# Layer norm behind a matmul: how the last row tile gets its shift

## The chip, the core and the metric

The kernel runs on one core of a Trainium2 chip. The metric is device time in microseconds of one launch. Three runs of the kernel before gave a median of 249.34 us (249.0 to 249.43).

## What is computed

A 2048x2048 matmul in fp32 inputs, and a layer norm over each row of the result:

```python
x = np.matmul(a, b)                              # 2048 x 2048 x 2048, fp32
mean = np.mean(x, axis=-1, keepdims=True)
var = np.var(x, axis=-1, keepdims=True)
normalized = (x - mean) / np.sqrt(var + eps)
return (gamma * normalized + beta).astype(np.float32)
```

## The kernel before

The 2048 output rows are sixteen row tiles of 128 rows. A row tile has four column blocks (q = 0 to 3) of 512 columns, and each is summed over sixteen k-tiles in one PSUM bank, with f16 copies of `a` (transposed) and `b` as operands. Everything is written in the order in which it is to run; there is no scheduler that moves work. Each engine takes its instructions in program order.

The first seven row tiles are worked on together while `b` arrives (blocks 1 and 0, then 2 and 3). From row tile 7 on, a row tile is finished before the next begins: `quarter` runs the sixteen products of a block, `evacuate` copies the bank to SBUF on ScalarE and takes the block's statistics on VectorE. `close` joins the statistics and puts the normalization into a backlog, which VectorE works off while TensorE goes on with the next tile.

The last row tile (15) has no next tile to hide behind, so it is treated apart. Its blocks 0 to 2 are multiplied by gamma as soon as they are there (`scaled`, L356), so that after the last product only `x*gamma*rstd + (beta - mean*rstd*gamma)` is left for them. Its block 3 isn't copied out of PSUM. After its last product, `finish_row` runs:

- `bn_stats` of block 3 from PSUM (L363), then in `stats` the aggregation into `mv` (mean, variance; L103), the addition of eps (`ve`, L105) and the square root on ScalarE (`sq`, L107).
- Eight products of zeros on TensorE (`filler`, L364 and L232).
- Block 3 centred and multiplied by gamma (L366), the reciprocal (`rstd`, L128), `nm = -mean*rstd` (L371).
- `nm`, a column of 128 values, is turned into a row by a product with a unit matrix (L374), copied by ScalarE into row 0 of `lead`, whose row 1 is ones (L375). Two products of two rows each (L379) then give `w[q] = nm*gamma + beta` for q = 1 and 2, in PSUM. Their moving operands, gamma above beta, are loaded into `rows_gb` earlier (L350).
- Block 3 is scaled and stored (L118, L124); for q = 0 VectorE itself computes `shift = gamma*nm + beta` (L384); then blocks 0, 1 and 2 get `x*rstd + w[q]` (L389) and are stored one by one by SP (L124).

All of these fp32 products appear in the trace as two matmul records each.

Of the kernel before, what the change touches and what calls it, by code (L numbers as in the profile page):

```python
# [9 lines left out]
FP32 = mybir.dt.float32  # L10
FP16 = mybir.dt.float16
AluOp = mybir.AluOpType
ActFn = mybir.ActivationFunctionType
# [3 lines left out]
def kernel(  # L17
# [9 lines left out]
    nc = tc.nc  # L27
    P = 128
# [5 lines left out]
    NB = 512  # L34
    n_nb = N // NB
    NH = N // 2
# [13 lines left out]
    konst = ctx.enter_context(tc.tile_pool(name="konst", bufs=1))  # L50
    bpool = ctx.enter_context(tc.tile_pool(name="bpool", bufs=1))
    stg = ctx.enter_context(tc.tile_pool(name="stg", bufs=6))
# [3 lines left out]
    stat = ctx.enter_context(tc.tile_pool(name="stat", bufs=8))  # L56
    psum = ctx.enter_context(tc.tile_pool(name="psum", bufs=8, space=bass.MemoryType.PSUM))
# [5 lines left out]
    eps_t = konst.tile([P, 1], FP32)  # L63
    gate = konst.tile([P, 1], FP32)
    gamma_b = konst.tile([P, N], FP32)
    beta_b = konst.tile([P, N], FP32)
# [3 lines left out]
    xs = [None] * n_mt  # L70
# [3 lines left out]
    def bank(name):  # L74
        return psum.tile([P, NB], FP32, tag="ps", name=name)
# [25 lines left out]
    def stats(i):  # L101
        mv = stat.tile([P, 2], FP32, tag="mv", name=f"mv{i}")
        nc.vector.bn_aggr(mv, bnst[i])  # L103
        ve = stat.tile([P, 1], FP32, tag="ve", name=f"ve{i}")
        nc.vector.tensor_tensor(ve, mv[:, 1:2], eps_t, AluOp.add)  # L105
        sq = stat.tile([P, 1], FP32, tag="sq", name=f"sq{i}")
        nc.scalar.activation(sq, ve, ActFn.Sqrt)  # L107
        return mv, sq

    def centre(i, q, mv):  # L110
# [5 lines left out]
    def scale(i, q, rstd):  # L116
        qs = ds(q * NB, NB)
        nc.vector.scalar_tensor_tensor(  # L118
            xs[i][:, qs], xs[i][:, qs], rstd, beta_b[:, qs],
            AluOp.mult, AluOp.add)  # L120

    def store(i, q0, nq):
        s = ds(q0 * NB, nq * NB)
        nc.sync.dma_start(out[ts(i, P), s], xs[i][:, s])  # L124

    def inv(i, sq):
        rstd = stat.tile([P, 1], FP32, tag="rstd", name=f"rstd{i}")
        nc.vector.reciprocal(rstd, sq)  # L128
        return rstd
# [100 lines left out]
    def filler(n, to=None):  # L230
        for _ in range(n):
            nc.tensor.matmul(warm if to is None else to, zeros[:, 0:P], zeros, start=True, stop=True)  # L232
# [22 lines left out]
    for what in arrivals:  # L255
# [9 lines left out]
        i = what[1]  # L265
# [73 lines left out]
        nc.gpsimd.dma_start(a16[i], a[ts(i, P), :])  # L339


    rows_gb = [stg.tile([2, 2, NB], FP32, tag="st", name=f"gb{h}") for h in (0, 1)]
    ident32 = stg.tile([P, P], FP32, tag="st", name="ident32")
    nc.vector.tensor_copy(ident32, ident)
    shift = stg.tile([P, NB], FP32, tag="st", name="shift")
    lead = konst.tile([2, P], FP32)
    nc.vector.memset(lead, 1.0)
    for h in (0, 1):
        for m, vec in enumerate((gamma, beta)):
            nc.sync.dma_start(  # L350
                rows_gb[h][m:m + 1, :, :],
                vec[ds(h * NH, NH)].rearrange("(o t n) -> o t n", o=1, t=2))

    def scaled(i, q):
        qs = ds(q * NB, NB)
# [2 lines left out]
    def finish_row(i):  # L358


        q3 = ds(3 * NB, NB)
        last_acc = acc[i, 3]
        nc.vector.bn_stats(bnst[i][:, 3, :], last_acc)  # L363
        filler(8, bank("warm2"))  # L364
        mv, sq = stats(i)
        nc.vector.scalar_tensor_tensor(  # L366
            xs[i][:, q3], last_acc, mv[:, 0:1], gamma_b[:, q3],
            AluOp.subtract, AluOp.mult)
        rstd = inv(i, sq)
        nm = stat.tile([P, 1], FP32, tag="nm", name="nm")  # L370
        nc.vector.scalar_tensor_tensor(  # L371
            nm, mv[:, 0:1], -1.0, rstd, AluOp.mult, AluOp.mult)
        nm_ps = psum.tile([1, P], FP32, tag="ps", name="nm_ps")
        nc.tensor.matmul(nm_ps, nm, ident32, start=True, stop=True)  # L374
        nc.scalar.copy(lead[0:1, :], nm_ps)  # L375
        w = {}
        for q in (1, 2):
            w[q] = bank(f"w{q}")
            nc.tensor.matmul(  # L379
                w[q], lead, rows_gb[q // 2][:, q % 2, :], start=True, stop=True)  # L380
        scale(i, 3, rstd)
        store(i, 3, 1)
        q0 = ds(0, NB)
        nc.vector.scalar_tensor_tensor(  # L384
            shift, gamma_b[:, q0], nm, beta_b[:, q0], AluOp.mult, AluOp.add)
        w[0] = shift
        for q in range(3):
            qs = ds(q * NB, NB)
            nc.vector.scalar_tensor_tensor(  # L389
                xs[i][:, qs], xs[i][:, qs], rstd, w[q], AluOp.mult, AluOp.add)  # L390
            store(i, q, 1)
# [5 lines left out]
    def close(i):  # L397
        mv, sq = stats(i)
        queue_norm(i, mv, sq)
        drain(1)  # L400
# [15 lines left out]
    for i in range(n_first, n_mt):  # L416
        last = i == n_mt - 1
        turn_ahead(i + 4)
        for q in range(2 if i < R else 0, n_nb):
            quarter(i, q)  # L420
            if last and q == n_nb - 1:
                break
            evacuate(i, q)
            if q < n_nb - 1:
                drain(1)
            if last:
                scaled(i, q)
        if last:
            drain(len(backlog))
            finish_row(i)  # L430
        else:
            close(i)
# [35 lines left out]
```

## Time and profile before

| | |
|---|---|
| median of three runs | 249.34 us (249.0 to 249.43) |
| the profiled execution | 249.5 us |
| its span, first to last instruction | 247.7 us |
| mean granted TensorE clock in it | 0.989 |
| TensorE busy with matmuls | 240.7 us (97%) |
| VectorE busy | 173.0 us (70%) |
| ScalarE busy | 56.9 us (23%) |

A profile is of one execution. Durations in it are microseconds from the span's start unless marked ns. "PE" is TensorE's matmuls, "PEld" its weight loads, DVE is VectorE, ACT is ScalarE, POOL is GpSimd, SP is the engine that issues the DMAs ("SPq" its queue). A group reads: line, engine, operation, output<-inputs, partitions x elements, type, count, then busy time and the mean ns of one, then the idle time of the engine ahead of it and what ended it. Matmuls are pipelined, so their records overlap, and a busy PE is not PE at its peak.

### The profile page before, as it was taken

Reading aid. Unit: us, or ns where it says so; the run is one execution under the profiler, and the core shown is the slowest. Engines: PE = TensorE matmul, PEld = TensorE weight load, DVE = VectorE, ACT = ScalarE, POOL = GpSimd, SP = SyncE. Lnnn points to the kernel's source line nnn. Section 1 sums busy time; section 2 is a strip of 40 time slices with the busy share of each in tenths; the row PEclk is TensorE's granted clock in tenths of the full one; section 3 lists DMA queues with packets and bytes.
Section 4 is the critical chain, followed back from the end, with each engine's and each line's share of the span. In section 5 each row is a group of like instructions: output and inputs, shape, how many; then the busy total and the mean of one; then the engine's idle time right before and its main releaser. Section 6 shows DMA issues by size and latency. Waiting matters only on the chain.

```text
span 247.7 us, 3055 instructions
## 1 busy us (share of the span) xinstructions
PE 240.7 (97%) x1175; PEld 110.5 (45%) x1175; DVE 173.0 (70%) x307; ACT 56.9 (23%) x101; POOL 5.6 (2%) x15
## 2 busy tenths in 40 slices
PE   8999999999999999999999999999999999999983
PEld 3445555444444444444444444444444444444430
DVE  1454555965799999999999492856658292947873
ACT  2276446400013312221112121212111121112100
POOL 0000000000030000000000000000000000000000
PEclk9999999999999999999999999999999999999995
DMA  5999999999999239999999979180903122120404
GB/s 147 331 390 385 379 363 389 387 386 385 390 350 210 99 128 221 201 281 252 120 285 324 252 186 266 68 219 3 253 1 125 47 85 85 67 102 3 171 0 169
DMA packets 37846, 52.64 MB, mean 213 GB/s; under 512 B 20292, under 2 KB 20292, under 8 KB 37576
## 3 DMA queue, kind: packets, MB, share of 16 engines
q1 hardware_dynamic: 36536, 47.73, 58.1%
q0 software_dynamic: 1296, 4.72, 12.0%
q8 instruction: 9, 0.15, 0.2%
q14 instruction: 5, 0.04, 0.1%
HBM read 35.67 MB, written 16.78 MB: 212 GB/s over the span
## 4 chain that ended last, share of the span: by engine, by line
PE 92%; DMA 3%; SPq 2%; DVE 1%; issue 0%; ACT 0%
PE acc L86 88%; DMA st<-in_a_dram 3%; PE tps L239 2%; PE w L379 1%; SPq L187 1%; SPq L201 1%; DVE x L389 0%; DVE bnst L363 0%; DVE x L366 0%; DVE a16s L189 0%; PE nm_ps L374 0%; DVE mv L103 0%; ACT lead L375 0%; DVE nm L371 0%; DVE ve L105 0%
## 5 line engine op out<-in xcount | busy, mean ns | idle before, releaser
L86 PE MATMUL acc<-b,at 128*128 128x512 f16 x1024 | 224.1, 379 | 0.0
L86 PEld LDWEIGHTS <-at 128*128 128x128 f16 x1024 | 99.5, 98 | 117.8 <-ACT at L241 1.1
L97 DVE BATCH_NORM_STATS2 bnst<-x 128x6 f32<-128x512 f32 x56 | 38.4, 687 | 36.7 <-ACT x L96 36.7
L96 ACT COPY x<-acc 128x512 f32<-128x512 f32 x56 | 32.7, 585 | 129.5 <-PE acc L86 129.4
L118 DVE SCALAR_TENSOR_TENSOR x<-x,rstd,beta_b 128x512 f32<-128x512 f32 x61 | 43.1, 748 | 0.5
L112 DVE SCALAR_TENSOR_TENSOR x<-x,mv,gamma_b 128x512 f32<-128x512 f32 x60 | 42.1, 744 | 0.0
L208 DVE CAST b<-stb 128x1024 f16<-128x1024 f32 x30 | 20.8, 692 | 14.9 <-DMA stb<-in_b_dram 14.5
L241 ACT COPY at<-tps 128x512 f16<-128x512 f16 (+1 forms) x19 | 15.0, 787 | 21.2 <-PE tps L239 21.2
L232 PE MATMUL warm<-zeros 128*128 128x512 f16 x33 | 11.0, 466 | 1.2 <-DVE zeros L153 1.2
L197 DVE CAST a16s<-sta 128x1024 f16<-128x1024 f32 x9 | 6.2, 694 | 6.1 <-DMA sta<-in_a_dram 6.1
L107 ACT ACTIVATE sq<-ve 128x1 f32<-128x1 f32 x16 | 3.2, 203 | 31.3 <-DVE ve L105 31.3
L239 PEld LDWEIGHTS <-a16s 128*128 128x128 f16 x112 | 7.6, 99 | 6.2 <-DVE a16s L189 2.9
L239 PE MATMUL tps<-ident,a16s 128*128 128x128 f16 x112 | 9.6, 222 | 0.6 <-DVE a16s L189 0.5
L189 DVE CAST a16s<-st 128x512 f16<-128x512 f32 x10 | 4.3, 425 | 6.3 <-DMA st<-in_a_dram 6.3
L339 POOL DMA_DIRECT2D a<-in_a_dram x9 | 4.9, 547 | 70.0 <-DMA at<-a 69.7
L232 PEld LDWEIGHTS <-zeros 128*128 128x128 f16 x33 | 3.5, 114 | 5.3 <-issue 2.4
L327 DVE BATCH_NORM_STATS2 bnst<-x 128x6 f32<-128x512 f32 x7 | 4.9, 695 | 0.2
L325 DVE TENSOR_TENSOR x<-acc,x 128x512 f32<-128x512 f32 x7 | 4.8, 681 | 0.0
L103 DVE BATCH_NORM_AGGREGATE mv<-bnst 128x2 f32<-128x24 f32 x16 | 4.2, 264 | 0.5
L297 ACT COPY x<-acc 128x512 f32<-128x512 f32 x7 | 3.5, 632 | 0.0
L202 DVE CAST b<-st 128x512 f16<-128x512 f32 x4 | 1.7, 428 | 2.3 <-DMA st<-in_b_dram 2.3
L105 DVE TENSOR_TENSOR ve<-mv,eps_t 128x1 f32<-128x1 f32 x16 | 2.6, 160 | 0.5
(26 smaller groups left out, 17.4 us busy)
## 6 DMA issues: line engine op xcount, KB each, us to landing
stb<-in_b_dram SPq DMA_DIRECT2D x30, 512.0 KB, 7.4
out_dram<-x SPq DMA_DIRECT2D x30, 512.0 KB, 3.0
sta<-in_a_dram SPq DMA_DIRECT2D x9, 512.0 KB, 7.5
a<-in_a_dram POOLq DMA_DIRECT2D x9, 512.0 KB, 8.0
st<-in_a_dram SPq DMA_DIRECT2D x10, 256.0 KB, 7.0
st<-in_b_dram SPq DMA_DIRECT2D x4, 256.0 KB, 5.8
gamma_b<-in_gamma_dram SPq DMA_DIRECT2D x1, 1024.0 KB, 9.4
beta_b<-in_beta_dram SPq DMA_DIRECT2D x1, 1024.0 KB, 11.3
```

Source lines behind the costliest of these rows:

```text
L86: nc.tensor.matmul(acc[i, q], at(i)[:, kt, :], b16[:, kt, ds(q * NB, NB)], start=first, stop=last,)
L96: nc.scalar.copy(xs[i][:, qs], acc[i, q])
L97: nc.vector.bn_stats(bnst[i][:, q, :], xs[i][:, qs])
L112: nc.vector.scalar_tensor_tensor(xs[i][:, qs], xs[i][:, qs], mv[:, 0:1], gamma_b[:, qs], AluOp.subtract, AluOp.mult)
L118: nc.vector.scalar_tensor_tensor(xs[i][:, qs], xs[i][:, qs], rstd, beta_b[:, qs], AluOp.mult, AluOp.add)
L197: nc.vector.tensor_copy(held["a"][:, ds(i % KC, 2), :], st)
L208: nc.vector.tensor_copy(b16[:, k:k + 2, ds(q * NB, NB)], st)
L232: nc.tensor.matmul(warm if to is None else to, zeros[:, 0:P], zeros, start=True, stop=True)
L239: nc.tensor.transpose(t_ps[:, m, j, :], a16_of[i, c][:, ts(j, P)], ident)
L241: nc.scalar.copy(pair[i0 // 2][:, ds(i0 % 2, n), ds(c * KC, KC), :], t_ps)
L327: nc.vector.bn_stats(bnst[p][:, 0, :], xs[p][:, 0:NB])
L339: nc.gpsimd.dma_start(a16[i], a[ts(i, P), :])
```

## The change

In `stats`, which all row tiles use, eps is no longer added by VectorE but given to the square root as its bias. In `finish_row` the fillers go. Ahead of the statistics' joining, TensorE gets two products of one row each that put beta into the banks of `w[1]` and `w[2]` and leave them open for accumulation. `nm` is laid on the diagonal of a 128x128 tile by ScalarE (a scaled copy of the unit matrix), and the product of that diagonal with gamma (128 rows deep) is added to the banks. The product that turned `nm` into a row, the copy into `lead` and the four loads of `rows_gb` are gone. The centring of block 3 is done in two halves, one ahead of the reciprocal and one behind `nm`. The last three blocks are finished in the order 1, 2, 0.

```diff
     def stats(i):
         mv = stat.tile([P, 2], FP32, tag="mv", name=f"mv{i}")
         nc.vector.bn_aggr(mv, bnst[i])
-        ve = stat.tile([P, 1], FP32, tag="ve", name=f"ve{i}")
-        nc.vector.tensor_tensor(ve, mv[:, 1:2], eps_t, AluOp.add)
         sq = stat.tile([P, 1], FP32, tag="sq", name=f"sq{i}")
-        nc.scalar.activation(sq, ve, ActFn.Sqrt)
+        nc.scalar.activation(sq, mv[:, 1:2], ActFn.Sqrt, bias=eps_t)
         return mv, sq
...
-    rows_gb = [stg.tile([2, 2, NB], FP32, tag="st", name=f"gb{h}") for h in (0, 1)]
     ident32 = stg.tile([P, P], FP32, tag="st", name="ident32")
     nc.vector.tensor_copy(ident32, ident)
     shift = stg.tile([P, NB], FP32, tag="st", name="shift")
-    lead = konst.tile([2, P], FP32)
-    nc.vector.memset(lead, 1.0)
-    for h in (0, 1):
-        for m, vec in enumerate((gamma, beta)):
-            nc.sync.dma_start(
-                rows_gb[h][m:m + 1, :, :],
-                vec[ds(h * NH, NH)].rearrange("(o t n) -> o t n", o=1, t=2))
+    diag = stg.tile([P, P], FP32, tag="st", name="diag")
+    ones = konst.tile([1, P], FP32)
+    nc.vector.memset(ones, 1.0)
...
         last_acc = acc[i, 3]
         nc.vector.bn_stats(bnst[i][:, 3, :], last_acc)
-        filler(8, bank("warm2"))
+        w = {0: shift}
+        for q in (1, 2):
+            w[q] = bank(f"w{q}")
+            nc.tensor.matmul(
+                w[q], ones, beta_b[0:1, ds(q * NB, NB)], start=True, stop=False)
         mv, sq = stats(i)
-        nc.vector.scalar_tensor_tensor(
-            xs[i][:, q3], last_acc, mv[:, 0:1], gamma_b[:, q3],
-            AluOp.subtract, AluOp.mult)
+
+        def centre_part(c0, c):
+            qs = ds(3 * NB + c0, c)
+            nc.vector.scalar_tensor_tensor(
+                xs[i][:, qs], last_acc[:, ds(c0, c)], mv[:, 0:1], gamma_b[:, qs],
+                AluOp.subtract, AluOp.mult)
+
+        centre_part(0, NB // 2)
         rstd = inv(i, sq)
         nm = stat.tile([P, 1], FP32, tag="nm", name="nm")
         nc.vector.scalar_tensor_tensor(
             nm, mv[:, 0:1], -1.0, rstd, AluOp.mult, AluOp.mult)
-        nm_ps = psum.tile([1, P], FP32, tag="ps", name="nm_ps")
-        nc.tensor.matmul(nm_ps, nm, ident32, start=True, stop=True)
-        nc.scalar.copy(lead[0:1, :], nm_ps)
-        w = {}
+        nc.scalar.mul(diag, ident32, nm)
         for q in (1, 2):
-            w[q] = bank(f"w{q}")
             nc.tensor.matmul(
-                w[q], lead, rows_gb[q // 2][:, q % 2, :], start=True, stop=True)
+                w[q], diag, gamma_b[:, ds(q * NB, NB)], start=False, stop=True)
+        centre_part(NB // 2, NB // 2)
         scale(i, 3, rstd)
         store(i, 3, 1)
-        q0 = ds(0, NB)
         nc.vector.scalar_tensor_tensor(
-            shift, gamma_b[:, q0], nm, beta_b[:, q0], AluOp.mult, AluOp.add)
-        w[0] = shift
-        for q in range(3):
+            shift, gamma_b[:, 0:NB], nm, beta_b[:, 0:NB], AluOp.mult, AluOp.add)
+        for q in (1, 2, 0):
             qs = ds(q * NB, NB)
```

## The prediction

> **What bounds the kernel now.** I read the page first. Its busy line and the row of the big product say that TensorE sets the time almost to the end; the clock row says that something happens to TensorE only in the last slice.
>
> ```profile
> span 247.7 us, 3055 instructions
> ...
> PE 240.7 (97%) x1175; PEld 110.5 (45%) x1175; DVE 173.0 (70%) x307; ACT 56.9 (23%) x101; POOL 5.6 (2%) x15
> ...
> PEclk9999999999999999999999999999999999999995
> ...
> L86 PE MATMUL acc<-b,at 128*128 128x512 f16 x1024 | 224.1, 379 | 0.0
> ```
>
> The chain that ended last shows one unbroken piece of L86 from 40.99 to 237.84. So what the change does in the other fifteen rows (one 0.16 us add less in each `stats`, L105) and at the start (four small loads fewer) lies beside TensorE's work and is worth nothing. Everything is decided after the last product, at 237.85. There the chain, asked for its last 10 us, goes on like this (start, duration, what):
>
> ```profile
> 240.14 0.39 PE nm_ps L374 x2
> 240.53 0.02 issue
> 240.55 0.26 ACT lead L375
> 240.81 0.04 issue
> 240.86 2.59 PE w L379 x4
> 243.45 0.03 issue
> 243.47 0.75 DVE x L389
> ```
>
> It ends through the two products `w` on TensorE: the last L389 waits for `w[2]`. The timeline of the same stretch gives VectorE's steps (start, duration):
>
> ```profile
> 237.87 0.70 DVE L363 BATCH_NORM_STATS2 bnst<-acc 128x6 f32<-128x512 f32 x1 [1.41 <-PE acc L86]
> ...
> 238.60 0.27 DVE L103 BATCH_NORM_AGGREGATE mv<-bnst 128x2 f32<-128x24 f32 x1
> 238.90 0.16 DVE L105 TENSOR_TENSOR ve<-mv,eps_t 128x1 f32<-128x1 f32 x1
> 238.98 0.74 DVE L366 SCALAR_TENSOR_TENSOR x<-acc,mv,gamma_b 128x512 f32<-128x512 f32 x1
> 239.16 0.20 ACT L107 ACTIVATE sq<-ve 128x1 f32<-128x1 f32 x1 [4.15 <-DVE ve L105]
> 239.64 0.15 DVE L128 RECIPROCAL rstd<-sq 128x1 f32<-128x1 f32 x1
> 239.83 0.16 DVE L371 SCALAR_TENSOR_TENSOR nm<-mv,rstd 128x1 f32<-128x1 f32 x1
> 239.91 0.74 DVE L118 SCALAR_TENSOR_TENSOR x<-x,rstd,beta_b 128x512 f32<-128x512 f32 x1
> ...
> 240.57 0.74 DVE L384 SCALAR_TENSOR_TENSOR shift<-gamma_b,nm,beta_b 128x512 f32<-128x512 f32 x1
> ```
>
> To be read here: an instruction that needs nothing of the one before it starts earlier than that one ends (239.91 to 240.57 is 0.66 for a row of 0.74); one that needs its result starts 0.03 to 0.04 after its end. So a 512-wide pass costs 0.66, or 0.78 ahead of a dependant; a one-column step costs 0.08, or 0.19. The square root was done at 239.36, but the reciprocal waited until 239.64 behind L366.
>
> VectorE could have begun the last L389 at 242.69 (the second began at 242.02) and began it at 243.47. Two rows tell why: a timeline answer for TensorE alone around 241.2, and the table by stretches (TensorE busy is the first figure after the length, the granted clock stands after POOL).
>
> ```profile
> 240.86 1.12 PE L379 MATMUL w<-gb,lead 2*128 2x512 f32 x2 [0.34 <-ACT lead L375]
> ```
>
> ```profile
> 238.70:242.11 3.41, 2.49 (x9) 0.97 (x8) 3.31 (x9) 0.46 (x2) 0.00 (x0) 1.00 0.18 67
> 239.56:242.11 2.55, 1.63 (x6) 0.78 (x6) 2.48 (x7) 0.25 (x1) 0.00 (x0) 1.00 0.24 90
> 242.11:243.45 1.34, 1.32 (x2) 0.00 (x0) 0.66 (x1) 0.00 (x0) 0.00 (x0) 0.50 0.44 162
> ```
>
> At full clock one `w` is ready 1.12 after its start (0.69 for the first pass, 0.43 for the second); the second `w` would follow 0.86 later, at 242.84. The clock fell to half at 242.11 and made that 243.45. At full clock the last step would have ended at 243.63 instead of 244.22: 0.59 of the profiled end is the clock.
>
> **The sum.** From the end of the last VectorE step (244.22) to the end of the span (247.70) there are 3.48 for the last store, and the profiled execution took 249.50, so 1.80 lie outside the span. This execution is 0.16 above the median of 249.34. A time below is therefore the end of the last L389 plus 5.28.
>
> Statistics and root. The add L105 goes; the root reads `mv` itself. It started 0.10 after the add's end, so now 0.10 after 238.87: 238.97 to 239.17. A bias read from a tile in place of a constant has no row; I take nothing, and 0.12 is free anyway, since the reciprocal comes later. Centring half 1 starts at 238.90. Its cost: 512 columns hold VectorE 0.66 and a one-column step 0.08, which on a straight line gives 0.37 for 256; with 0.02 for caution 0.39. The reciprocal starts at 239.29 instead of 239.64, `nm` at 239.48 and ends at 239.64. That is 0.35 earlier.
>
> Diagonal. Removed from the path: the product L374 and the copy L375, that is from the end of `nm` (239.99) to the start of `w` (240.86), 0.87. In their place ScalarE writes 128x128. Its bounds are 0.20 (128x1, L107) and 0.59 (128x512, L96); a straight line gives 0.30 and I take that. Start 0.10 after `nm`: 239.74 to 240.04, TensorE at 240.09. This is 0.77 earlier than before; at the upper bound 0.48.
>
> The products with gamma. Four passes of 512 fp32 columns as before, but 128 rows deep instead of 2. L374 streams a 128-row fp32 operand twice 128 columns wide in 0.39, of which an isolated f16 product of that width takes 0.22, so depth shows no surcharge. Its weights, 128x128 fp32, have no row: L379's 2x128 took 0.18, the f16 128x128 0.10. I take 0.18; were it 0.36, both `w` come 0.18 later (later loads hide behind 0.43 passes) and the end is about 0.2 later, 249.0. The Trainium skill ("TensorE: Matmul & The Clock Gate", LDWEIGHTS) has a load depend on columns and not on rows, which would make that surcharge nothing. So `w[1]` is ready at 241.21 and `w[2]` at 242.07.
>
> The beta products. Two fp32 products of one row stand ahead, four passes of 0.43 from 237.85: done at 239.56, or 239.73 with the drain. The eight fillers that they replace ended at 239.56. Nothing on the path waits for them; cover is 0.36 to 240.09. At half clock they would end near 241.4 and push both `w` by 1.3.
>
> VectorE to the end. Half 2 of the centring starts behind `nm` at 239.56, and its full length is 0.74 less 0.27, so 0.47: 240.03. `scale` L118 needs it, 240.07; it ends 0.16 later than before, and so the first store, which has three others behind it. The shift starts at 240.73, and since the next step no longer needs it, that one may start at 241.39. Column block 1: 241.39 (`w[1]` has been ready 0.18). Block 2: 242.06 by VectorE, 242.11 by `w[2]`. Block 0: 242.78, ending at 243.53. The stores follow 0.67 apart; SP needs 0.33 for one, and before, the two at 242.13 and 242.79 were as close, so I charge nothing, up to 0.1. Against 244.22 that is 0.69: **248.81**, 0.53 (0.2%) below the median. About 0.6 of it is the clock avoided and only 0.1 the shorter path: VectorE itself has no gap left.
>
> **The rivals.**
>
> *The clock falls during the products (slower).* Before, eight f16 products kept TensorE streaming until 239.56, and 2.55 later the clock was cut although the rows have it busy for 1.63 of that. If narrow fp32 work counts little as load, the changed kernel's load ends at 237.85 and the same 2.55 gives a cut at 240.41, inside the products. Checked on before: 0.56 of streaming left at 242.11 (242.84 less a drain of 0.17: an f16 record lasts 0.38, the next follows after 0.21) doubled predicts 243.40, measured 243.45. With a cut at 240.41, `w[1]` comes at 241.84 and `w[2]` at 243.56; block 2 starts at 243.60, block 0 at 244.27, end 245.02: 250.3, slower by 0.9. It decides from a cut before about 241.2: then `w[2]` is at 242.77 and the end where it was. For it: one-row products replace full ones. Against: if fp32 work counts as busy, only 0.5 of idle time is left between 237.85 and 242.07, where 0.92 was.
> The Trainium skill (same page, The HAM clock gate) says that the clock is decided in free-running windows of about 3.4 us, and is cut after an idle one. The trace agrees on the grid: the first fillers start 0.43 apart until about 6.6 and 0.22 after it, and 242.11 less 6.6 is 69 such windows; it disagrees on "idle", with 2.49 busy of the last 3.41. By that grid the decisions here fall at 238.70 and 242.11, the second just behind my products: 248.8. As the page has the grid at another place in every execution, it would also allow 250.3.
>
> *Nothing measurable.* Where before's clock falls late, before ends at 243.63 and gains only 0.10. Likewise a cut at 241.2 in the changed kernel. Time 249.0 to 249.5. For it: the three runs span 0.43, which is less than the clock's 0.59. Against: the median stands 0.4 above such an unhindered run (249.50 less 0.59 is 248.91).
>
> *ScalarE loads a table for the scaled copy.* L107 shows one load of 1.28, none between its sixteen roots and the copies around them. If the scaling brought one, `w[2]` would be ready at 243.35 and the end 244.8, 250.1. A small chance.
>
> *The change doesn't shorten the root's wait* because the reciprocal still stands behind a half of the centring: included, 0.05 at most.
>
> **How the numbers follow.** A measurement of this kernel can tell about 0.2%, 0.5 us, from no change. Forecast (clock holds): 0.62, of which 0.47 beyond that bound and 0.15 within, as 0.53 hardly passes it. Cut during the products: 0.22, of which 0.20 slower and 0.02 within. Nothing measurable: 0.12 (0.03, 0.08, 0.01). Table load: 0.04, slower. Sums: 0.50, 0.25, 0.25. Range: from 248.4, which is the forecast less the 0.43 by which the three runs differ, up to 250.0, which takes in the dearer weights, the late cut and about half of the early ones; some 0.15 to 0.2 lies outside.
>
> **What would show it.** Right: no L105; the reciprocal near 239.3 if the last product ends at 237.85; `w` with gamma starting 0.45 after `nm` ends; three passes of block 1, 2, 0 at 0.67 spacing with no wait on TensorE; the granted clock 1.00 until past 242.0; last step ending 243.5. Wrong: a wait of block 2 on `w`, with the clock row at 0.50 earlier; TensorE still on beta after 240; a table load at the scaled copy; a diagonal that takes 0.5.

## The result and the profile after

The changed kernel takes 250.78 us (median of 20 runs, 248.94 to 251.91); the kernel before, measured beside it, 249.09 (248.34 to 250.06). The ratio is 1.006 with a 95% interval of 1.0046 to 1.0075: slower by 0.6%, where 0.2% faster was forecast. The median hides two groups. Twelve of the twenty have a mean granted TensorE clock of 0.990 or less (below, such a run is called cut) and take 250.5 to 251.9; the other eight have 0.995 to 0.998 and take 248.9 to 249.7. So two questions are to be answered: why the first group exists, and why the second is not at 248.8.

The profiled execution took 250.9 and belongs to the first group. Its page begins:

```profile
span 248.9 us, 3024 instructions
...
PEclk9999999999999999999999999999999999999987
```

The chain behind the last big product (start, duration, what):

```profile
237.75 0.71 DVE bnst L356
...
239.37 0.17 DVE nm L373
239.54 0.02 issue
239.56 0.41 ACT diag L375
239.97 0.04 issue
240.02 3.57 PE w L377 x4
243.59 0.02 issue
243.61 0.75 DVE x L386
244.36 0.66 DVEq L460
```

Up to the start of the products with gamma it goes as forecast: 237.75 to 240.02 is 2.27 (forecast 237.87 to 240.09, 2.22). Then the four passes take 3.57 instead of the 1.98 of full clock. The timeline shows what VectorE makes of it (the last column is its wait):

```profile
241.91 0.75 DVE L386 SCALAR_TENSOR_TENSOR x<-x,rstd,w 128x512 f32<-128x512 f32 x1 [0.53 <-PE w L377]
243.61 0.75 DVE L386 SCALAR_TENSOR_TENSOR x<-x,rstd,w 128x512 f32<-128x512 f32 x1 [0.96 <-PE w L377]
```

Against the sum of the prediction, the 2.09 too few in this execution (250.90 less 248.81) lie here:

| part | forecast | measured | difference |
|---|---|---|---|
| last big product ends at | 237.83 | 237.71 | -0.12 |
| from there to the end of the last VectorE step | 5.70 | 7.31 | +1.61 |
| from there to the end of the span | 3.48 | 3.91 | +0.43 |
| outside the span | 1.80 | 1.96 | +0.16 |

The last two rows are in the second group of runs as well. Of the changed kernel run again, the profiled execution kept its clock (249.54). Its timeline is the forecast one: products with gamma in 1.98, no waits worth naming, and the last step ending 5.74 behind the last big product (forecast 5.70). Behind that step it still takes 3.93 to the end of the span and 2.00 outside it:

```profile
239.72 0.40 ACT L375 ACTIVATE diag<-ident,nm 128x128 f32<-128x128 f32 x1 [0.43 <-DVE nm L373]
...
240.18 1.98 PE L377 MATMUL w<-gamma_b,diag 128*128 128x512 f32 x4 [0.40 <-ACT diag L375]
...
242.87 0.75 DVE L386 SCALAR_TENSOR_TENSOR x<-x,rstd,shift 128x512 f32<-128x512 f32 x1
```

### The profile page after: what moved, and what is told of

It reads as the page before. It is cut to its first block, busy times and chain, and to the rows that moved or that the text cites. A ratio compares the mean times of both kernels' runs of the same rounds, so it can differ in the third digit from the quotient of the medians.

```text
span 248.9 us, 3024 instructions
## 1 busy us (share of the span) xinstructions
PE 240.9 (97%) x1169; PEld 110.5 (44%) x1169; DVE 170.4 (68%) x292; ACT 58.9 (24%) x101; POOL 5.6 (2%) x15
## 4 chain that ended last, share of the span: by engine, by line
PE 92%; DMA 3%; SPq 2%; DVE 1%; issue 0%; DVEq 0%; ACT 0%
PE acc L86 88%; DMA st<-in_a_dram 3%; PE tps L237 2%; PE w L377 1%; SPq L185 1%; SPq L199 1%; DVE x L386 0%; DVE bnst L356 0%; DVEq L460 0%; DVE x L366 0%; DVE a16s L187 0%; ACT diag L375 0%; DVE mv L103 0%; DVE nm L373 0%; DVE rstd L126 0%
## 5 line engine op out<-in xcount | busy, mean ns | idle before, releaser
L105 ACT ACTIVATE sq<-mv,eps_t 128x1 f32<-128x1 f32 x16 | 4.7, 295 | 22.5 <-DVE mv L103 22.5
L230 PE MATMUL warm<-zeros 128*128 128x512 f16 x25 | 8.5, 463 | 1.2 <-DVE zeros L151 1.2
L230 PEld LDWEIGHTS <-zeros 128*128 128x128 f16 x25 | 2.6, 114 | 4.5 <-issue 2.4
L377 PE MATMUL w<-gamma_b,diag 128*128 128x512 f32 x4 | 3.6, 1045 | 0.4 <-ACT diag L375 0.4
```

Of the source, the lines that this page charges most:

```text
L377: nc.tensor.matmul(w[q], diag, gamma_b[:, ds(q * NB, NB)], start=False, stop=True)
```

## Experiments on the clock

**The changed kernel once more**, without an edit.

> The changed kernel once more, for its spread beside the others. Theory N (one-row fp32 products do not count as load, so the clock is cut at the first 3.41 us window that holds too little of the wide work before 237.8): some runs near 249.4, where the cut falls behind the products, and more of them at 250.5 to 251.9, where it falls inside; median 250 to 251. Rival F (any fp32 product counts little): the same. Rival S (the loss is the order of the stores at the end, not the clock): all runs within 0.5 of one another.

Measured: 249.56 (248.86 to 250.74), ratio 1.0021 (1.0003 to 1.0038). The runs are 1.88 apart, so rival S falls. Three of twelve were cut, against twelve of twenty in the first set. A third time (below) it was five of six, 250.59. So the loss of a set of runs depends on how many of them are cut; in all, 20 of 38 were. Two of the three here, at 249.65 and 249.81, stand close to the uncut ones; the prediction has a cut behind about 241.2 come too late to cost anything.

**Only the depth of the beta products** (e1_deep_beta): as many passes, the same values in the banks.

```diff
-                w[q], ones, beta_b[0:1, ds(q * NB, NB)], start=True, stop=False)
+                w[q], ident32, beta_b[:, ds(q * NB, NB)], start=True, stop=False)
```

> Only the depth of the beta products is changed: the 128-row unit matrix times the broadcast beta in place of one row of ones times one row of beta; same passes, same results. Theory N: now all the work counts, no window ahead of the products' end is poor, so no run above 250, median 248.8 to 249.4, granted clock 1.00 until past 242. Rival F (fp32 as such counts little): as the changed kernel, 250.8 median, clock cut inside the products. Rival S (stores): as the changed kernel.

Measured: 249.63 (249.12 to 250.46), ratio 1.0027 (1.001 to 1.0043), all twelve clocks 0.994 or more. The forecast of the clock held, that of the time (248.8 to 249.4) did not: there is a loss that isn't the clock.

**The kernel before with narrow fillers** (e2_before_narrow):

```diff
-        filler(8, bank("warm2"))
+        warm2 = bank("warm2")
+        for q in (1, 2):
+            nc.tensor.matmul(
+                warm2, lead[0:1, :], beta_b[0:1, ds(q * NB, NB)], start=True, stop=True)
```

> The kernel before with its eight f16 fillers replaced by two one-row fp32 products of the same length (four passes), results unused. Theory N: the clock is cut up to 1.7 us earlier, inside the two products of w; median 0.5 to 1.5 above the kernel before, single runs up to 252. Rival F: the same as theory N. Rival S: unchanged, 249.1.

Measured: 249.85 (248.41 to 250.55), ratio 1.0026 (1.0006 to 1.0047), nine of twelve clocks at 0.990 or less, where the kernel before beside it had 3 of 35. That is 0.65 above the kernel before by the ratio and 0.86 by the medians, inside the 0.5 to 1.5 of theory N; no run came near 252.

The tables by stretches of these kernels settle what counts. Each stretch is the 3.41 us ahead of a place where the clock could change. The first figure after the length is TensorE's busy time; the third from the end is the clock granted in the stretch itself, so what was decided at its end stands in the line below. First the changed kernel (cut at 240.28):

```profile
236.87:240.28 3.41, 3.01 (x9) 1.12 (x8) 2.39 (x7) 0.70 (x2) 0.00 (x0) 1.00 0.00 0
240.28:243.70 3.42, 3.29 (x4) 0.71 (x3) 1.93 (x4) 0.00 (x0) 0.00 (x0) 0.50 0.26 98
243.70:247.11 3.41, 0.00 (x0) 0.00 (x0) 1.32 (x2) 0.00 (x0) 0.00 (x0) 1.00 0.59 210
```

Then e1_deep_beta, whose clock was kept behind the first of these two stretches:

```profile
237.89:241.30 3.41, 2.82 (x8) 1.04 (x7) 3.12 (x8) 0.70 (x2) 0.00 (x0) 1.00 0.00 0
241.30:244.72 3.42, 0.99 (x3) 0.16 (x1) 2.43 (x4) 0.00 (x0) 0.00 (x0) 1.00 0.64 235
```

And e2_before_narrow:

```profile
240.31:243.72 3.41, 3.17 (x4) 1.16 (x4) 2.19 (x4) 0.19 (x1) 0.00 (x0) 0.50 0.41 154
243.72:247.13 3.41, 0.61 (x1) 0.00 (x0) 0.75 (x1) 0.00 (x0) 0.00 (x0) 0.50 0.41 154
```

TensorE is busy for 3.01 of 3.41 with one-row products among it, and the clock is cut; it is busy for 2.82 with 128-row products, and the clock is kept. At half clock, 3.29 of 128-row products bring it back to 1.00 (243.70); 3.17 of two-row products do not (243.72). So narrow fp32 products keep TensorE busy but count for little or nothing as load, while fp32 as such counts: rival F of the expectations falls.

The profiled execution of e3_order (next) makes it sharper. TensorE is busy for 3.01 there too, from 238.42 to 241.83, and the clock is kept; 1.62 of it is 128-row products, next to 1.10 in the cut stretch of the changed kernel. That the values count instead (a row of ones against a unit matrix) doesn't fit: in the changed kernel the clock rose at 4.76, when TensorE had run nothing but products of zeros.

Six kernels with the 128-row beta products and the three f16 versions below had no clock under 0.992 in 99 runs.

**The order 1, 0, 2** (e3_order):

```diff
-        for q in (1, 2, 0):
+        for q in (1, 0, 2):
```

> The changed kernel with the last blocks in the order 1, 0, 2 instead of 1, 2, 0: block 0, whose shift needs no product, is done while w[2] is still being computed. Theory N: where the clock is cut inside the products, the end comes 0.67 earlier (the pass of block 0 fits into the wait of 0.96); where it isn't, nothing changes; median 250.2 to 250.5. Rival S: the stores stand further apart, the gain is in all runs alike, 0.3 or more.

Measured: 250.06 (249.68 to 251.56), ratio 1.0053 (1.0036 to 1.007). Its profiled execution wasn't cut; the last step ended 5.64 behind the last big product, 0.10 less than in the other order. Four of twelve runs were cut, and what they gain can't be told from these numbers. Rival S's gain in all runs is not there. Instead 0.33 more lies outside the span (median 2.41 against 2.08), for which see the next section. As a test of the order it is inconclusive.

## Experiments on the loss that is not the clock

Here four times of the last store are compared, read from the trace: its issue, its landing (the last of its semaphore events), the end of the span and the run's end. "Outside" is the median over the runs of time less span; "fetch" is the start of the last 8 KB code fetch (a DMA packet that brings instructions), counted from the end of the span. "SP" is the number of SP's records, that is the length of its program.

| kernel | issue to landing | landing to end | outside | SP | fetch |
|---|---|---|---|---|---|
| before | 2.45 | 1.00 | 1.76 | 207 | +1.00 |
| changed | 2.64 | 1.25 | 2.08 | 202 | +1.86 |
| e1_deep_beta | 2.67 | 1.25 | 2.09 | 202 | +1.87 |
| e2_before_narrow | 2.45 | 1.02 | 1.80 | 207 | +1.03 |
| e3_order | 2.76 | 1.25 | 2.41 | 201 | +2.21 |
| e4_loads_back | 2.65 | 1.01 | 1.79 | 208 | +0.54 |
| e7_before_more_loads | 2.44 | 1.73 | 1.78 | 213 | -0.30 |
| e12_loads_by_act | 2.66 | 1.00 | 2.10 | 202 | +1.88 |
| e14_eight_loads | 2.66 | 1.73 | 1.78 | 211 | -0.22 |

Three things are longer in the changed kernel. *Issue to landing* is 0.2 to 0.3 longer wherever the last two stores are 0.66 apart (in e2_before_narrow the last one is issued 1.70 behind the one ahead of it, in before 1.45). *Landing to end:* behind the last store SP waits for its DMA semaphores one by one in a fixed order, each wait 0.06 behind the one before. In before the last store lands on the sixth of eight, in the changed kernel on the second. The line of SP's last drains shows the end of that round; first before, then the changed kernel:

```profile
L463 SPq DRAIN  x3: 7/7/7, 246.9 to 247.2; - x3
```

```profile
L460 SPq DRAIN  x3: 7/7/7, 248.1 to 248.4; - x3
```

The landings were at 246.70 and 247.69, so it is 0.2 in the one and 0.4 in the other. *Outside* is taken up below.

**The four loads put back** (e4_loads_back, on e1_deep_beta; the tile of ones, which nothing reads any more, is gone in this and the later versions with 128-row beta products):

```diff
+    rows_gb = [stg.tile([2, 2, NB], FP32, tag="st", name=f"gb{h}") for h in (0, 1)]
...
+    for h in (0, 1):
+        for m, vec in enumerate((gamma, beta)):
+            nc.sync.dma_start(
+                rows_gb[h][m:m + 1, :, :],
+                vec[ds(h * NH, NH)].rearrange("(o t n) -> o t n", o=1, t=2))
```

> e1_deep_beta with the four small loads of gamma and beta put back; nothing reads what they bring. Theory W (at the end SP waits for its DMA semaphores one by one in a fixed order, 0.06 us each; four loads fewer let the last store land on a semaphore that stands four places earlier in that order): the time from the last store's landing to the end of the span falls from 1.25 to 1.00, so the median falls by 0.25 against e1_deep_beta. Rival (the longer tail is the crowding of the last stores): 1.25 stays, no change.

Measured: 249.30, ratio 0.9996 (0.998 to 1.0012), against 1.0027 for e1_deep_beta. 1.01 behind the landing, as theory W says; and the time outside fell to 1.79, which it did not foretell. By these two times, loads that nothing reads are worth 0.54 here.

**The additions put back** (e5_adds_back, on e1_deep_beta), and **both** (e6_both_back):

```diff
+        if i == n_mt - 1:
             nc.scalar.activation(sq, mv[:, 1:2], ActFn.Sqrt, bias=eps_t)
+        else:
+            ve = stat.tile([P, 1], FP32, tag="ve", name=f"ve{i}")
+            nc.vector.tensor_tensor(ve, mv[:, 1:2], eps_t, AluOp.add)
+            nc.scalar.activation(sq, ve, ActFn.Sqrt)
```

> e1_deep_beta with the addition of eps put back on VectorE in the first fifteen row tiles; the last one keeps the bias. Theory C (the time outside the span is longer because VectorE's shorter program ends just ahead of a boundary at which 8 KB of code are fetched, so the fetch that the kernel before made at 232 us now comes after the last instruction): a fetch near 232 in the trace again, the time outside the span falls from 2.07 to about 1.76, the median by 0.3 against e1_deep_beta. Rival (the time outside belongs to the last stores or to SP): 2.07 stays. The path behind the last product is the same in both.

> e4_loads_back and e5_adds_back together: the path of the changed kernel with 128-row beta products, the loads and the additions of before. Theories W and C: 0.55 below e1_deep_beta, 248.6 to 249.1, level with or 0.1 to 0.4 below the kernel before. Rivals: as e1_deep_beta, about 249.6.

Measured: e5_adds_back 249.50, ratio 1.0009 (0.9991 to 1.0026); a code fetch at 231.8 is there again, and the time outside is 2.05. Theory C has fallen: VectorE's fetch and the time outside have nothing to do with one another. e6_both_back 249.30, ratio 0.9996 (0.998 to 1.0013), the same as e4_loads_back. The additions are worth nothing, as forecast.

**The kernel before with eight loads instead of four** (e7_before_more_loads; the second four go to tiles of their own, unread):

```diff
     for h in (0, 1):
         for m, vec in enumerate((gamma, beta)):
...
+            nc.sync.dma_start(
+                idle_gb[h][m:m + 1, :, :],
+                vec[ds(h * NH, NH)].rearrange("(o t n) -> o t n", o=1, t=2))
```

> The kernel before with the four small loads doubled to eight, the second four unread. Theory W: the last store lands four semaphores on, so the time from its landing to the end of the span is 1.25 instead of 1.00 and the median 0.25 above the kernel before. Rival (crowded stores): 1.00, no change.

Measured: 250.10, ratio 1.0038 (1.002 to 1.0055). The store lands on the second semaphore, as foretold, but 1.73 instead of 1.25 lie behind it. Most of the 0.48 is one step of SP among its last waits, 0.40 long instead of 0.06 (246.79 to 247.19), and a code fetch now starts inside the span, at 247.83. The pause ends 0.64 ahead of the fetch's packet, and from the packet on SP is as quick as in before (0.45 from its last drain to its last wait, 0.44 there). So the pause comes with the fetch, but the packet itself is not what SP stands still for; what it is stays open.

**The changed kernel and the four loads, nothing else** (e10_after_third without an edit, e11_after_loads with the edit of e4_loads_back on the changed kernel):

> The changed kernel a third time, beside the next one. Time outside the span 2.07; from the last store's landing to the end of the span 1.25; some runs with a granted clock of 0.990 or less (cut inside the products), the rest near 249.5.

> The changed kernel, one-row beta products kept, with the four small loads put back, unread. Theory W plus theory D (the time outside the span is SP's: its shorter program reaches the boundary of an 8 KB code fetch later behind the kernel's end): 1.00 instead of 1.25 behind the landing, 1.78 instead of 2.07 outside, so 0.55 below the changed kernel at the same clock; the share of cut clocks unchanged. Rival (VectorE's program sets the time outside): 2.07 stays and only 0.25 is gained.

Measured side by side: 250.59, ratio 1.0063 (1.0042 to 1.0084), and 248.95, ratio 1.001 (0.9995 to 1.0025). In e11_after_loads 1.01 lie behind the landing (246.09 to 247.10) and 1.86 outside. Five of six and five of eleven runs were cut, so the medians differ by more than the loads are worth; the uncut runs of e11_after_loads take 248.4 to 249.0.

**Turn or length** (on e1_deep_beta: the four loads issued by ScalarE, and eight loads on SP):

```diff
-            nc.sync.dma_start(
+            nc.scalar.dma_start(
```

```diff
+            for _ in (0, 1):
                 nc.sync.dma_start(
```

> e4_loads_back, but the four unread loads are issued by ScalarE's queue, so SP's program is as short as in the changed kernel. Theory D (the time outside the span follows the length of SP's program): 2.07 outside again. Rival (it follows the semaphore on which the last store lands, or the loads themselves): 1.78 outside. The time from the last landing to the end of the span tells by itself whether loads of another queue move the semaphores: 1.00 if so, 1.25 if not.

> e1_deep_beta with eight unread loads on SP instead of four: a whole turn of the eight semaphores, so the last store lands where it does with none, but SP's program is longer. Theory W: 1.25 behind the landing again, and as in e7_before_more_loads perhaps 0.5 more where the code fetch falls inside the span. Theory D: 1.78 outside, not 2.07. Rival for both (a load count as such gives the gain): 1.00 and 1.78.

Measured: e12_loads_by_act 249.01, ratio 0.9995 (0.9975 to 1.0014), 1.00 behind the landing and 2.10 outside. Loads of another queue turn the semaphores just as well, but the time outside stays with SP's short program. e14_eight_loads 249.82, ratio 1.0027 (1.0007 to 1.0048): a whole turn, the store on the second semaphore again, 1.73 behind the landing and 1.78 outside. The fetch is inside the span again, and again one step of SP is long (0.38, between two of its drains) and ends 0.64 ahead of the packet. Theory W holds: 1.00 or 1.01 with four loads, 1.25 with none, and in e14_eight_loads 0.49 from the landing to the start of the first drain, next to 0.45 with none, ahead of the long step. What theory D says is seen in all kernels of the table: the shorter SP's program, the later the fetch behind the end, and where it starts as late as +1.86 the run ends later too. That the fetch is the cause is inferred from this alone.

## Versions that take the second step further

**An f16 diagonal and a third bank** (e8_f16_diag, on e4_loads_back): VectorE's pass for `shift` goes.

```diff
+    gamma16 = stg.tile([P, 3 * NB], FP16, tag="st", name="gamma16")
+    diag = stg.tile([P, P], FP16, tag="st", name="diag")
...
-        for q in (1, 2):
+        for q in (1, 2, 0):
...
+        nc.scalar.mul(diag, ident, nm)
...
+                w[q], diag, gamma16[:, ds(q * NB, NB)], start=False, stop=True)
```

> e4_loads_back with the diagonal and gamma in f16 and a third bank, so that all three blocks take their shift from TensorE and VectorE's shift pass is gone; the term -mean*rstd*gamma is rounded to f16. A one-pass f16 product costs 0.22 where the fp32 one costs 0.86: all three w are there by 241.3 and VectorE loses a pass of 0.66. Expected 0.7 below e4_loads_back by trace (5.0 from the last big product to the last VectorE step instead of 5.74), median 0.5 to 0.8 below the kernel before, whatever the clock does. Rival (the stores, now 0.66 apart behind one another, give it back): at most 0.3 gained.

Measured: 248.72, ratio 0.9992 (0.9975 to 1.0009). The path is as expected, 4.97 instead of 5.74, but of the 0.5 to 0.8 below the kernel before only 0.27 came; the rival's bound of 0.3 held. Three products take 0.81 together, and VectorE runs through:

```profile
240.08 0.81 PE L381 MATMUL w<-gamma,diag 128*128 128x512 f16 x3
240.58 2.06 DVE L388 SCALAR_TENSOR_TENSOR x<-x,rstd,w 128x512 f32<-128x512 f32 x3
```

Of the gain, 0.2 goes to the landing (2.83 from issue to landing, with four stores 0.66 apart) and 0.35 lies outside the span (2.14), although SP has 207 records and the fetch starts at +1.01, as in before.

**The last block in two halves** (e9_f16_split) and **a fifth load** (e13_f16_five), both on e8_f16_diag:

```diff
+            for c in (0, NB // 2):
+                cs = ds(c, NB // 2)
+                nc.vector.scalar_tensor_tensor(
+                    xs[i][:, cs], xs[i][:, cs], rstd, w[q][:, cs], AluOp.mult, AluOp.add)
+                nc.sync.dma_start(out[ts(i, P), cs], xs[i][:, cs])
```

```diff
+    nc.sync.dma_start(
+        rows_gb[0][0:1, :, :],
+        gamma[ds(0, NH)].rearrange("(o t n) -> o t n", o=1, t=2))
```

> e8_f16_diag with the last block done and stored in two halves of 256 columns. If the last store's landing is set by its size, it lands 0.2 to 0.3 earlier after its issue, against 0.13 more on VectorE: 0.1 to 0.2 below e8_f16_diag. Rival (the stores stand in a queue, so smaller ones end no sooner, and one more semaphore and one more issue come on top): the same or 0.1 slower.

> e8_f16_diag with a fifth unread small load on SP. Theory D: SP's program is one load longer and the 2.14 outside fall to about 1.78; the last store lands on the next semaphore, 0.06 less behind the landing; median 0.4 below e8_f16_diag against the same kernel before. Rival (the 2.14 of e8_f16_diag has nothing to do with SP): 2.14 stays.

Measured: e9_f16_split 248.63 (248.11 to 249.20), ratio 0.9983 (0.997 to 0.9996): the only version whose interval lies wholly below the kernel before. Its path is 0.13 longer, its time from issue to landing (242.68 to 245.62, 2.94) not shorter; what it gains is outside the span, 1.78. So the reason in the expectation is wrong, the rival is right on the stores, and the gain has another source. e13_f16_five 248.75, ratio 0.9986 (0.9965 to 1.0006): landing to end 0.96, as expected, but 2.16 outside with 208 records and the fetch at +0.53, as its rival has it. So theory D doesn't cover e8_f16_diag and e13_f16_five; what lies outside the span there stays open.

## Why the prediction was wrong, step by step

- *What bounds the kernel.* Right. The other fifteen row tiles are worth nothing (e5_adds_back, e6_both_back).
- *Statistics, root, centring in halves.* Right in sum. The reciprocal starts 1.43 behind L356's start (forecast 1.42). Within it, the root with a bias from a tile takes 0.29 instead of 0.20, which the prediction set at nothing; its cover of 0.12 held.
- *Diagonal.* Forecast 0.10 of wait and 0.30; measured 0.03 and 0.40. Together right.
- *Products with gamma.* Right at full clock (1.98). A load of 128x128 fp32 weights takes 0.19, next to 0.18 for 2x128. The Trainium skill's rule ("TensorE: Matmul & The Clock Gate", LDWEIGHTS), columns and not rows, agrees.
- *Beta products.* The length was right (done 1.91 behind the last big product, forecast 1.88), and so nothing waits for them. The failed step is the assumption of the likeliest case that they count as load like the fillers they replace ("if fp32 work counts as busy, only 0.5 of idle time is left"). That was given 0.62. The rival priced the other case: a cut at 240.41, the last step ending at 245.02, 250.3. Measured: a cut at 240.28, and 245.02; the time was 250.90, for the constant below. Its mechanism was right and its chance of 0.22 too small. That the place agreed so well is luck: it counted 2.55 from the end of the load, but in e10_after_third the cut came at 241.23, 3.15 behind the last big product, and the last step ended 6.73 behind it instead of 7.31. The trace of before already spoke: TensorE was busy for 2.49 of 3.41 there and was cut, with 0.86 of f16 fillers and 0.38 of L374 in it; the rest was narrow.
- *The grid.* In the changed kernel the clock rose at 4.76 and fell at 240.28, again 69 steps of 3.41, but 1.83 earlier than in before. So the sentence of the prediction that relied on the same place (decisions at 238.70 and 242.11) did not hold. The Trainium skill ("TensorE: Matmul & The Clock Gate", The HAM clock gate) has the place of the windows differ from execution to execution, and the traces agree. It has the clock cut after an idle window; the measurement differs: a stretch that is 88% busy (3.01 of 3.41) with mostly narrow products is cut.
- *The clock avoided* ("About 0.6 of it is the clock avoided"). The 0.59 was read from one execution of the kernel before, which was cut (0.989), and taken off a median of three runs. Of the 124 runs of that kernel that were measured beside the experiments, only 23 have a clock of 0.990 or less, so a typical run had little of it to lose; the median of twenty is 249.09, not 249.34. Even e4_loads_back and e6_both_back, never cut and with the loads in place, are level with the kernel before (0.9996) and not 0.5 below it.
- *The stores* ("I charge nothing, up to 0.1"): mis-sized, 0.19 in the profiled execution.
- *A constant behind the last step* ("plus 5.28"): the failed assumption, in all runs. The four small loads "at the start" were set at nothing beside TensorE's work. They cost no time where they ran, but without them 0.25 was lost at the end, by the semaphore on which the last store lands, and 0.3 outside the span, which goes with the length of SP's program.

With the loads put back and the clock kept, the changed kernel's profiled execution takes 248.95 (e11_after_loads), 0.14 above the 248.81 of the sum. Part of that nearness is luck, since its last big product ended 0.17 earlier than the sum has it; the path behind it is 0.04 too short in the sum, and what follows the last step 0.27. The sum of the path was right; the constants, the clock and what the kernel before had to lose by it were not.

## What to carry to other kernels

Work put on TensorE to hold its clock must be as deep as the real work: look at the stretch ahead of the cut for what ran, not for how long it was busy. When the gain hoped for is below 1 us, the end of the program is part of the sum: which semaphore the last store lands on, where the last code fetch falls, and how closely the last stores follow one another. Removing instructions anywhere on the queue that ends the program can move all three, so measure an edit there with the old count of loads beside it.

## What was not expected of the hardware

The load that keeps the clock: in the 3.41 us ahead of a decision, 1.24 us of 128-row work were too little (0.86 of fillers and 0.38 of L374 in before; 1.29 in e7_before_more_loads, cut at 241.74), and 1.62 were enough (e3_order), as were 1.98 (the changed kernel run again, 239.57 to 242.98, busy for 2.19). This gives an estimate of how often the changed kernel is cut, if narrow work counts for nothing and the places of the stretches are evenly spread. With the times of its profile, a stretch that ends between 239.83 and 241.31 holds less than 1.29 of such work, and one that ends between 239.50 and 241.64 less than 1.62. That is 1.5 to 2.1 of every 3.41, or 43 to 63%; 20 of 38 runs are 53%.

Where an 8 KB code fetch by SP starts just ahead of the end, the span is 0.48 longer (1.73 against 1.25), by a step of SP that stands still ahead of the fetch's packet. How SP's program acts on time outside the span is only inferred from where the fetch falls; e8_f16_diag and e13_f16_five show that it is not all.
